# Four Strassen pairs instead of three in the last projection of an encoder trunk, two of each pair's weight sums made by adding DMA transfers

## The chip, the cores and the metric

One core of a Trainium2 chip runs the whole program. The metric is device time in microseconds of one launch, the median of several runs. TensorE (PE) multiplies, VectorE (DVE) and ScalarE (ACT) do the element-wise work, GpSimd (POOL) and SyncE (SP) issue transfers here, and 16 DMA engines carry them out.

## The reference, cut to what matters

Two layers, 256 tokens, model width 2048, all in float32. Each layer projects the normed input into conv, differential-attention and memory-attention heads, and projects the gated head outputs back:

```python
for l in range(DEPTH):                       # DEPTH = 2
    h = rmsnorm(x, norm_g[l])
    proj = h @ w_in[l]
    ...
    y = jnp.concatenate([y_a, y_d, y_m], axis=-1) @ w_out[l]   # (256 x 2048) @ (2048 x 2048)
    x = x + y
```

The last line but one, for l = 1, is where the change works. y has 16 column groups of 128: 0 to 5 from the conv, 6 to 11 from six differential heads, 12 to 15 from four memory heads.

## The kernel before

**Products.** float32 products are made of parts: every weight and every token tile is split into a rounded part (hi, on ScalarE) and a remainder (lo, on VectorE), and a product is three matmuls, hi x hi, hi x lo and lo x hi (lines 301 to 307, 348 to 351). Tokens are the stationary side, in two tiles of 128; 512 weight columns stream. A weight tile of two row blocks by 512 columns (512 KB) is loaded on SP's queue into one of four raw buffers and split into one of four pairs of hi and lo buffers (`load_w`, 286 to 296); it feeds 2 row blocks x 2 token tiles x 3 = 12 matmuls.

**The last projection.** w_out has four column blocks of 512. Blocks 0 and 1 run first over the head groups, with their accumulators left open (1222), and then over the six conv groups (1244 to 1247). Blocks 2 and 3 are done together: `near` accumulates block 2, `far` block 3 (1253, 1291, 1293).

**The Strassen pairs.** For a pair of row blocks k and k+1, two token tiles and the column blocks 2 and 3, the 2 x 2 x 2 product is done with seven products instead of eight (Winograd's form). The four token sums are made ahead by `token_sums` (353 to 366), on VectorE, once the heads that they need are there (`all_sums`, 1203 to 1209). `seven` (368 to 409) loads the two row blocks, each over both column blocks (128 x 1024, 512 KB), on SP; splits B11; makes four weight sums in place on VectorE (line 380, four calls); splits each side; and issues the products. Three go into accumulators that the ordinary tiles share (`near` twice, `far` once), four into accumulators of their own (`x`), which `collect` (1256 to 1280) adds up after the last pair, in steps between later weight tiles. Layer 0 has two pairs; layer 1 has three, ahead of the near block's tiles at positions 2, 6 and 8 of ten remaining row blocks (1249). In layer 1 all weight sums live in the buffers tagged "sh" and "e".

**Order.** Instructions passed to `pin` stay in program order among themselves on their engine; the others are placed by a scheduler at compile time. Each engine then runs its instructions in that fixed order, and so does each queue. `run_side` steps the side tasks once for each weight tile; `later(g, n)` makes a task due n such steps on. `leave(1)` adds column block 1's accumulators to the residual; it is called from inside the first pair (`meanwhile`), and the far accumulators use the same four PSUM buffers in rotation, so they wait for it.

**Buffers that the change takes.** "bgT" holds the conv's gate until the last conv group is multiplied by it (1170); "mqT" and "ga" hold the conv's turned input (1157); "bgx" its source sheet; "mv" the memory values.

Of the kernel before, what the change touches and what calls it, by code (L numbers as in the profile page):

```python
# [10 lines left out]
F32 = mybir.dt.float32  # L11
# [3 lines left out]
ALU = mybir.AluOpType  # L15
# [33 lines left out]
def encoder(ctx: ExitStack, tc: tile.TileContext, x, mem, norm_g, w_in, conv_w, conv_b,  # L49
# [21 lines left out]
    def nm(s):  # L71
        uid[0] += 1
        return f"{s}_{uid[0]}"
# [235 lines left out]
    def block(stat, w, cols, order, steps=1, apart=0, acc=None, more=False, rows=row_tiles, ready=None,  # L309
              opened=None, between={}):  # L310


        opened = opened or (acc is not None,) * NT
        if acc is None:
            acc = accumulators()
        n = len(order)

        def ends(k, t):
            return k == order[0] and not opened[t], k == order[-1] and not more

        late = []
        for c in range(0, n, CK):
            if c in between:
                between[c](acc)
            k0 = order[c]
            parts = ready(c // CK) if ready else load_w(rows(w, k0), cols)
            for j in range(CK):
                k = k0 + j
                settle(stat, k)
                for t in range(NT):  # L330
                    if t > 0 and c >= n - apart:
                        late.append((t, k, *parts[j]))
                    else:
                        products(stat, acc[t], t, k, *parts[j], *ends(k, t))
            run_side(steps)
        whole = late[:-SPLIT] if apart else late
        for t, k, hi, lo in whole:
            products(stat, acc[t], t, k, hi, lo, *ends(k, t))
        if apart:
            near, far = slice(0, NB // 2), slice(NB // 2, NB)  # L340
            for t, k, hi, lo in late[-SPLIT:]:
                products(stat, acc[t][:, near], t, k, hi[:, near], lo[:, near], *ends(k, t))
            acc.append(ps_acc.tile([P, NB // 2], F32, tag="acc", name=nm("rest")))
            for i, (t, k, hi, lo) in enumerate(late[-SPLIT:]):
                products(stat, acc[-1], t, k, hi[:, far], lo[:, far], i == 0, i == SPLIT - 1)
        return acc

    def product(left, acc, right, first, last):

        for i, (a, b) in enumerate(((0, 0), (0, 1), (1, 0))):  # L350
            nc.tensor.matmul(acc, left[a], right[b], start=first and i == 0, stop=last and i == 2)  # L351

    def token_sums(stat, k, home):

        f = tmp.tile([P, 2, SEQ], F32, tag="nat", name=nm("f"), bufs=3)
        pin(nc.vector.tensor_tensor(f, stat[:, 0, k:k + 2, :].bitcast(F32), stat[:, 1, k:k + 2, :].bitcast(F32), ALU.add))
# [3 lines left out]
        pin(nc.vector.tensor_tensor(s[:, 0], a21, a22, ALU.add))  # L360
        pin(nc.vector.tensor_tensor(s[:, 2], a11, a21, ALU.subtract))
        pin(nc.vector.tensor_tensor(s[:, 1], s[:, 0], a11, ALU.subtract))
        pin(nc.vector.tensor_tensor(s[:, 3], a12, s[:, 1], ALU.subtract))
        yield 1
        pin(nc.scalar.copy(home[:, 0], s))
        pin(nc.vector.tensor_tensor(home[:, 1], s, home[:, 0].bitcast(F32), ALU.subtract))

    def seven(stat, k, sums, w, col0, c_near, c_far, x, first, last, homes, meanwhile):


        a, b = (pl.tile([P, 2, NB], F32, tag=tag, name=nm("wide")) for pl, tag in homes)
        for j, raw in enumerate((a, b)):
            pin(nc.sync.dma_start(raw.rearrange("p j c -> p (j c)"), w[(k + j) * P:(k + j + 1) * P, col0:col0 + 2 * NB]))

        def split(src, to=None):
            hi, lo = to or parts_tiles()
            return ((hi, pin(nc.scalar.copy(hi, src))), (lo, pin(nc.vector.tensor_tensor(lo, src, hi.bitcast(F32), ALU.subtract))))  # L377

        def minus(dst, v, u):
            pin(nc.vector.tensor_tensor(dst, v, u, ALU.subtract))  # L380

        def side_of(parts, j):
            return [v[:, j] for v, _ in parts]

        one = keep.tile([P, 2, 1, NB], F32R, tag="mga", name=nm("one"))
        b11 = split(a[:, 0:1], (one[:, 0], one[:, 1]))
        minus(a[:, 0], a[:, 1], a[:, 0])
        minus(a[:, 1], b[:, 1], a[:, 1])
        b2 = split(b)
        minus(b[:, 1], b[:, 1], a[:, 0])  # L390
        minus(b[:, 0], b[:, 0], b[:, 1])
        meanwhile()
        t13 = split(a)
        t42 = split(b)

        def tokens(j, t):
            return [stat[:, part, k + j, t * P:(t + 1) * P] for part in range(2)]

        def summed(i):
            return [sums[:, part, i] for part in range(2)]  # L400

        x1, x5, x6, x7 = x
        product(tokens(0, 0), x1, side_of(b11, 0), first, last)
        product(tokens(1, 0), c_near[0], side_of(b2, 0), False, False)
# [3 lines left out]
        product(tokens(1, 1), c_near[1], side_of(t42, 0), False, False)  # L408
        product(summed(1), x6, side_of(t42, 1), first, last)

    def row_stats(ss, tag):
# [651 lines left out]
    for l in range(DEPTH):  # L1063
# [137 lines left out]
        sums = []  # L1201

        def all_sums(l, yT, sums):
            for n, tag in enumerate(("mkT0", "v") if l + 1 < DEPTH else ("mkT0", "mkT1", "v")):
                while tag == "v" and (l, MH // 2 - 1) not in summed_heads:
                    yield 1
                sums.append(keep.tile([P, 2, 4, P], F32R, tag=tag, name=nm("sums")))
                yield from token_sums(yT, CG + 2 * n, sums[n])
                yield 1
# [29 lines left out]
        def leave(b, acc, keep_order=lambda i: i, n=5):  # L1239
            finish(b, acc, keep_order)  # L1240
            if not final:
                tasks.append(later(x_next(xT, l + 1, b), n))

        for b in range(2):
            block(yT, w_out[l], [(b * NB, NB)], convs, acc=accs[b])
            if b == 0:
                leave(b, accs[b])

        places = (2, 6, 8) if final else (2, 6)
        paired = [CG + 2 * n for n in range(len(places))]  # L1250
        homes = [((tmp, tag),) * 2 for tag in ("sh", "e", "sh")] if final else [((tmp, "sh"),) * 2, ((keep, "bgx"), (keep, "ga"))]
        rest = [k for k in heads + convs if not CG <= k < CG + 2 * len(places)]
        near, far = accumulators(), accumulators()
        x = [pl.tile([P, NB], F32, tag=tag, name=nm("x")) for pl, tag in ((ps_s, "s"), (ps_s, "s"), (ps_t, "t"), (ps_t, "t"))]

        def collect(near):

            def at(t, b):
                return xs[:, t, b * NB:(b + 1) * NB]

            def plus(dst, v, u):
                pin(nc.vector.tensor_tensor(dst, v, u, ALU.add))

            x1, x5, x6, x7 = x
            u, v = (tmp.tile([P, NB], F32, tag="nat", name=nm("u"), bufs=3) for _ in range(2))
            pin(nc.scalar.copy(u, x1))
            plus(at(0, 2), u, at(0, 2))
            plus(u, u, x6)
            plus(v, u, x7)
            yield 1  # L1270
            plus(at(1, 2), v, at(1, 2))
            if not final:
                leave(2, near, n=3)
            plus(u, u, x5)
            plus(at(0, 3), u, at(0, 3))
            yield 1
            plus(v, v, x5)
            plus(at(1, 3), v, at(1, 3))
            if final:
                leave(2, near)  # L1280

        def pair_at(n):
            def run(near):
                seven(yT, paired[n], sums[n], w_out[l], 2 * NB, near, far, x, n == 0, n == len(paired) - 1,
                      homes[n], (lambda: leave(1, accs[1], pin, 4)) if n == 0 else lambda: None)
                if n == len(paired) - 1:
                    tasks.append(later(collect(near), 5))
                run_side(1)
            return run

        block(yT, w_out[l], [(2 * NB, NB)], rest, acc=near, opened=(False, False),
              between={c: pair_at(n) for n, c in enumerate(places)})
        acc = block(yT, w_out[l], [(3 * NB, NB)], rest, apart=4 if final else 0, acc=far, opened=(True, False))
        leave(3, acc)
# [31 lines left out]
```

## Time and profile before

| what | us |
|---|---|
| runs (three): median; lowest to highest | 918.98; 918.62 to 919.94 |
| the profiled execution: whole time | 919.16 |
| the profiled execution: span from first to last instruction | 917.4 |
| TensorE busy in the span | 911.9 |
| VectorE busy | 720.1 |
| ScalarE busy | 515.8 |
| GpSimd busy | 38.3 |

Matmuls overlap one another: each shows about 0.39 us, while a new one starts every 0.23 us, so the pace is read from long unbroken rows and not from single durations. Times in rows of a timeline are microseconds from the start of the span; a row gives start, length, engine, line, operation, output and inputs, shapes, count, and in brackets the idle time before it with what ended it.

### The profile page before, as it was taken

To read this page: it belongs to the slowest core of one execution; us is meant where nothing else is said; L and a number is where in the kernel's file an instruction comes from. 1 tells how busy PE (TensorE), PEld (TensorE's weight loads), DVE (VectorE), ACT (ScalarE), POOL (GpSimd) and SP (SyncE) were. 2 spreads that over 40 slices of the span, in tenths; PEclk is the share of its full clock that TensorE was granted. 3 is DMA by queue.
4 is the path that set the end of the run, shared out by engine and by line. 5 is a ranking of instruction groups with operands and counts; after the bars stand their busy time and mean duration, and the time that the engine had idled before them with its cause. 6 is when DMAs were issued, how large, how long until landed. Compare 5 with 4: busy or idle time off the path is not lost.

```text
span 917.4 us, 12407 instructions
## 1 busy us (share of the span) xinstructions
PE 911.9 (99%) x4161; PEld 757.3 (83%) x4161; DVE 720.1 (78%) x1293; ACT 515.8 (56%) x798; POOL 38.3 (4%) x68
## 2 busy tenths in 40 slices
PE   9999999999999999999999999999999999999998
PEld 6888888888888888888888888888888888888887
DVE  5579978857799697677789857878898787588786
ACT  5667645675555556445556544578555565546352
POOL 2435010000000000000000000000000000000000
PEclk9999999999999999999999999999999999999999
DMA  8899878886679998979777867986889998968842
GB/s 288 289 243 248 287 247 229 244 222 197 188 206 238 247 256 235 263 243 241 264 215 228 275 203 213 268 239 178 236 231 221 266 260 227 268 215 234 275 161 92
DMA packets 244560, 215.15 MB, mean 235 GB/s; under 512 B 131976, under 2 KB 171720, under 8 KB 244496
## 3 DMA queue, kind: packets, MB, share of 16 engines
q1 hardware_dynamic: 239520, 208.71, 79.3%
q0 software_dynamic: 3776, 4.59, 2.1%
q10 hardware_dynamic: 1200, 1.07, 0.3%
q8 instruction: 32, 0.52, 0.2%
q14 instruction: 32, 0.26, 0.1%
HBM read 193.30 MB, written 21.00 MB: 234 GB/s over the span
## 4 chain that ended last, share of the span: by engine, by line
PE 99%; DMA 0%; ACT 0%; SPq 0%; DVE 0%; issue 0%; ACTq 0%
PE acc L305 92%; PE x L351 2%; PE po L519 1%; PE acc L351 1%; PE s L627 1%; PE po L749 1%; PE s L626 1%; PE acc L933 1%; PE pt L763 0%; DMA raw<-in_w_mem_kv_dram 0%; PE s L683 0%; PE s L681 0%; PE s L682 0%; PE rest L305 0%; ACT hi L915 0%; SPq L833 0%
## 5 line engine op out<-in xcount | busy, mean ns | idle before, releaser
L305 PE MATMUL acc<-hi,xT 128*128 128x512 f32 x1792 | 558.4, 390 | 0.0
L294 ACT CAST hi<-raw 128x1024 fp32r<-128x1024 f32 x270 | 283.9, 1053 | 277.3 <-PE acc L305 200.0
L295 DVE TENSOR_TENSOR lo<-raw,hi 128x1024 fp32r<-128x1024 f32 x270 | 329.0, 1222 | 126.7 <-ACT hi L294 124.5
L305 PEld LDWEIGHTS acc<-hi,xT 128*128 128x128 f32 x1792 | 336.3, 188 | 69.0
L305 PE MATMUL acc<-lo,xT 128*128 128x512 f32 x896 | 349.2, 390 | 0.0
L305 PEld LDWEIGHTS acc<-lo,xT 128*128 128x128 f32 x896 | 168.2, 188 | 33.6
L305 PE MATMUL acc<-hi,yT 128*128 128x512 f32 (+1 forms) x432 | 134.1, 388 | 0.0
L305 PEld LDWEIGHTS acc<-hi,yT 128*128 128x128 f32 x432 | 81.0, 188 | 16.7
L305 PE MATMUL acc<-lo,yT 128*128 128x512 f32 x216 | 83.7, 388 | 0.0
L305 PE MATMUL acc<-hi,memT 128*128 128x512 f32 x248 | 78.0, 392 | 0.0
L305 PEld LDWEIGHTS acc<-hi,memT 128*128 128x128 f32 x248 | 46.2, 188 | 9.3
L916 DVE SCALAR_TENSOR_TENSOR lo<-raw,cva,hi 128x1024 fp32r<-128x1024 f32 (+1 forms) x34 | 41.0, 1218 | 15.4 <-ACT hi L915 15.1
L305 PE MATMUL acc<-lo,memT 128*128 128x512 f32 x124 | 48.0, 391 | 0.0
L305 PEld LDWEIGHTS acc<-lo,yT 128*128 128x128 f32 x216 | 40.6, 188 | 8.4
L915 ACT ACTIVATE hi<-raw,cva 128x1024 fp32r<-128x1024 f32 (+1 forms) x34 | 36.5, 1101 | 12.4 <-DMA raw<-in_w_mem_kv_dram 12.2
L305 PEld LDWEIGHTS acc<-lo,memT 128*128 128x128 f32 x124 | 23.3, 188 | 5.5 <-DVE lo L916 0.8
L377 ACT CAST hi<-wide 128x1024 fp32r<-128x1024 f32 x15 | 15.6, 1050 | 16.3 <-DVE wide L380 6.9
L637 ACT ACTIVATE e<-e,mx 128x256 f32<-128x256 f32 x48 | 23.8, 500 | 1.4 <-DVE mx L633 1.3
L780 POOL DMA_DIRECT2D xt<-in_x_dram x32 | 21.5, 678 | 19.7 <-DVE rsy L189 13.6
L377 DVE TENSOR_TENSOR lo<-wide,hi 128x1024 fp32r<-128x1024 f32 x15 | 18.1, 1220 | 3.5 <-ACT hi L377 3.3
L264 ACT ACTIVATE xT<-xf,gx 128x256 fp32r<-128x256 f32 x32 | 14.3, 503 | 5.7 <-DVE xf L786 5.0
L631 DVE SCALAR_TENSOR_TENSOR e<-dist,s 128x512 f32<-128x512 f32 x24 | 15.7, 680 | 2.2 <-PE s L627 1.7
(210 smaller groups left out, 765.8 us busy)
## 6 DMA issues: line engine op xcount, KB each, us to landing
raw<-in_w_in_dram SPq DMA_DIRECT2D x192, 512.0 KB, 4.6
raw<-in_w_out_dram SPq DMA_DIRECT2D x54, 512.0 KB, 4.8
raw<-in_w_in_dram SPq DMA_DIRECT2D x64, 256.0 KB, 4.3
raw<-in_w_mem_kv_dram SPq DMA_DIRECT2D x30, 512.0 KB, 6.4
d<-sh SPq DMA_DIRECT2D x88, 128.0 KB, 4.2
sh<-d SPq DMA_DIRECT2D x72, 128.0 KB, 4.1
wide<-in_w_out_dram SPq DMA_DIRECT2D x10, 512.0 KB, 7.0
xs<-in_x_dram SPq DMA_DIRECT2D x4, 512.0 KB, 6.3
```

The lines of the kernel that those rows point to most:

```text
L264: both = (nc.scalar.activation(hi, src, AF.Copy, scale=gain), nc.vector.scalar_tensor_tensor(lo, src, gain, hi.bitcast(F32), ALU.mult, ALU ...
L294: nc.scalar.copy(hi, raw)
L295: nc.vector.tensor_tensor(lo_, raw, hi.bitcast(F32), ALU.subtract)
L305: i = nc.tensor.matmul(acc, left, right, start=start, stop=stop)
L351: nc.tensor.matmul(acc, left[a], right[b], start=first and i == 0, stop=last and i == 2)
L377: return ((hi, pin(nc.scalar.copy(hi, src))), (lo, pin(nc.vector.tensor_tensor(lo, src, hi.bitcast(F32), ALU.subtract))))
L519: nc.tensor.matmul(po[:, t, :], eT[:, i, t, k, :], v[:, k, h * P:(h + 1) * P], start=k == 0, stop=k == NT - 1)
L631: nc.vector.scalar_tensor_tensor(e[:, c], dist, -slopes[h], s[c], ALU.mult, ALU.add)
L637: nc.scalar.activation(e[:, c, i], e[:, c, i], AF.Exp, bias=mx[:, c, i:i + 1], accum_out=sm[:, c, i:i + 1])
L780: tc.keep_in_program_order(nc.gpsimd.dma_start(st[:, n], src[n * B:(n + 1) * B].rearrange("p (b r) -> b p r", b=NA)))
L915: both = (nc.scalar.activation(hi[:, j], raw[:, j], AF.Copy, scale=g), nc.vector.scalar_tensor_tensor(lo[:, j], raw[:, j], g, hi[:, j].bit ...
L916: nc.vector.scalar_tensor_tensor(lo[:, j], raw[:, j], g, hi[:, j].bitcast(F32), ALU.mult, ALU.subtract))
```

## The change

- **Signs.** In both layers the token sums and the weight sums change sign, so that all four weight sums are additions: B11 + B12, B12 + B22, B22 + (B11 + B12), B21 + (B22 + B11 + B12). `collect` subtracts where it added.
- **Adding transfers, layer 1 only.** A new function `load_pair` loads a pair. In layer 1 it also copies B11 to a place of its own on SP's queue, and GpSimd issues a transfer of B12 and B22 that adds them to the loaded B11 and B12. `seven` then makes only two sums there.
- **A fourth pair, layer 1 only**: row blocks 12 and 13, the first two memory heads, whose token sums go to "mv". The pairs stand at positions 0, 2, 4 and 6 of eight remaining row blocks.
- **Earlier loads, layer 1 only.** The first pair's loads stand ahead of column block 1's conv tiles; each pair loads the next one's. The buffers are "sh", "e", "bgx" and "ga", and "sh" again; the copies of B11 go to "bgT" and "mqT".
- **Order inside the first pair.** It opens the near accumulators, and `leave(1)` comes after the splits of the sums instead of ahead of them. `collect` is due three steps after the last pair, not five.

```diff
 def token_sums(stat, k, home):
...
-        pin(nc.vector.tensor_tensor(s[:, 0], a21, a22, ALU.add))
+        pin(nc.vector.tensor_tensor(s[:, 0], a21, a22, ALU.subtract))
...
-        pin(nc.vector.tensor_tensor(s[:, 3], a12, s[:, 1], ALU.subtract))
+        pin(nc.vector.tensor_tensor(s[:, 3], a12, s[:, 1], ALU.add))
...
-    def seven(stat, k, sums, w, col0, c_near, c_far, x, first, last, homes, meanwhile):
-        a, b = (pl.tile([P, 2, NB], F32, tag=tag, name=nm("wide")) for pl, tag in homes)
+    def load_pair(k, w, col0, homes):
+
+        a, b = (h[:, 0:2] for h in homes[:2])
         for j, raw in enumerate((a, b)):
             pin(nc.sync.dma_start(raw.rearrange("p j c -> p (j c)"), w[(k + j) * P:(k + j + 1) * P, col0:col0 + 2 * NB]))
+        if len(homes) > 2:
+            pin(nc.sync.dma_start(homes[2][:, 0], w[k * P:(k + 1) * P, col0:col0 + NB]))
+            pin(nc.gpsimd.dma_start(a, w[k * P:(k + 2) * P, col0 + NB:col0 + 2 * NB].rearrange("(j p) c -> p j c", p=P),
+                                    accum_op=ALU.add))
+
+    def seven(stat, k, sums, c_near, c_far, x, first, last, opens, homes, meanwhile):
...
-        b11 = split(a[:, 0:1], (one[:, 0], one[:, 1]))
-        minus(a[:, 0], a[:, 1], a[:, 0])
-        minus(a[:, 1], b[:, 1], a[:, 1])
+        b11 = split(homes[2] if len(homes) > 2 else a[:, 0:1], (one[:, 0], one[:, 1]))
+        if len(homes) == 2:
+            plus(a[:, 0], a[:, 0], a[:, 1])
+            plus(a[:, 1], a[:, 1], b[:, 1])
         b2 = split(b)
-        minus(b[:, 1], b[:, 1], a[:, 0])
-        minus(b[:, 0], b[:, 0], b[:, 1])
-        meanwhile()
+        plus(b[:, 1], b[:, 1], a[:, 0])
+        plus(b[:, 0], b[:, 0], b[:, 1])
+        if not opens:
+            meanwhile()
         t13 = split(a)
         t42 = split(b)
+        if opens:
+            meanwhile()
...
-            for n, tag in enumerate(("mkT0", "v") if l + 1 < DEPTH else ("mkT0", "mkT1", "v")):
-                while tag == "v" and (l, MH // 2 - 1) not in summed_heads:
+            for n, tag in enumerate(("mkT0", "v") if l + 1 < DEPTH else ("mkT0", "mkT1", "v", "mv")):
+                while tag in ("v", "mv") and (l, MH // 2 - 1) not in summed_heads:
...
+        places = (0, 2, 4, 6) if final else (2, 6)
+        paired = [CG + 2 * n for n in range(len(places))]
+        rest = [k for k in heads + convs if not CG <= k < CG + 2 * len(places)]
+        copies = []
+
+        def homes(n):
+            def home(pl, tag, j=2):
+                return pl.tile([P, j, NB], F32, tag=tag, name=nm("wide"))
+
+            ab = (home(keep, "bgx", 3), home(keep, "ga", 3)) if n == len(paired) - (2 if final else 1) else \
+                [home(tmp, "e" if final and n == 1 else "sh") for _ in range(2)]
+            if not final:
+                return ab
+            if n == 0:
+                copies.extend((home(keep, "bgT", 3), home(keep, "mqT")))
+            return *ab, copies[n // 3][:, n % 3:n % 3 + 1]
+
+        loaded = []
+
+        def load_next():
+            if len(loaded) < len(paired):
+                loaded.append(homes(len(loaded)))
+                load_pair(paired[len(loaded) - 1], w_out[l], 2 * NB, loaded[-1])
+
         for b in range(2):
+            if final and b:
+                load_next()
             block(yT, w_out[l], [(b * NB, NB)], convs, acc=accs[b])
...
-        places = (2, 6, 8) if final else (2, 6)
-        paired = [CG + 2 * n for n in range(len(places))]
-        homes = [((tmp, tag),) * 2 for tag in ("sh", "e", "sh")] if final else [((tmp, "sh"),) * 2, ((keep, "bgx"), (keep, "ga"))]
-        rest = [k for k in heads + convs if not CG <= k < CG + 2 * len(places)]
...
-            plus(u, u, x5)
+            minus(u, x5, u)
...
-            plus(v, v, x5)
+            minus(v, x5, v)
...
         def pair_at(n):
             def run(near):
-                seven(yT, paired[n], sums[n], w_out[l], 2 * NB, near, far, x, n == 0, n == len(paired) - 1,
-                      homes[n], (lambda: leave(1, accs[1], pin, 4)) if n == 0 else lambda: None)
+                load_next()
+                seven(yT, paired[n], sums[n], near, far, x, n == 0, n == len(paired) - 1,
+                      places[n] == 0, loaded[n], (lambda: leave(1, accs[1], pin, 4)) if n == 0 else lambda: None)
                 if n == len(paired) - 1:
-                    tasks.append(later(collect(near), 5))
+                    tasks.append(later(collect(near), 3 if final else 5))
...
-        block(yT, w_out[l], [(2 * NB, NB)], rest, acc=near, opened=(False, False),
+        block(yT, w_out[l], [(2 * NB, NB)], rest, acc=near, opened=(places[0] == 0,) * NT,
               between={c: pair_at(n) for n, c in enumerate(places)})
```

More of the change, by code (lines that the diff above doesn't have):

```diff
@@ L366, in token_sums @@
         pin(nc.vector.tensor_tensor(home[:, 1], s, home[:, 0].bitcast(F32), ALU.subtract))
-    def seven(stat, k, sums, w, col0, c_near, c_far, x, first, last, homes, meanwhile):
-        a, b = (pl.tile([P, 2, NB], F32, tag=tag, name=nm("wide")) for pl, tag in homes)
+    def load_pair(k, w, col0, homes):
+        a, b = (h[:, 0:2] for h in homes[:2])
         for j, raw in enumerate((a, b)):
             pin(nc.sync.dma_start(raw.rearrange("p j c -> p (j c)"), w[(k + j) * P:(k + j + 1) * P, col0:col0 + 2 * NB]))
+        if len(homes) > 2:
[3 more added lines that the diff above has]
+    def seven(stat, k, sums, c_near, c_far, x, first, last, opens, homes, meanwhile):
+        a, b = (h[:, 0:2] for h in homes[:2])
         def split(src, to=None):
@@ L377, in split, with plus @@
             return ((hi, pin(nc.scalar.copy(hi, src))), (lo, pin(nc.vector.tensor_tensor(lo, src, hi.bitcast(F32), ALU.subtract))))
-        def minus(dst, v, u):
-            pin(nc.vector.tensor_tensor(dst, v, u, ALU.subtract))
+        def plus(dst, v, u):
+            pin(nc.vector.tensor_tensor(dst, v, u, ALU.add))
         def side_of(parts, j):
@@ L403, in seven @@
         product(tokens(0, 0), x1, side_of(b11, 0), first, last)
-        product(tokens(1, 0), c_near[0], side_of(b2, 0), False, False)
+        product(tokens(1, 0), c_near[0], side_of(b2, 0), opens, False)
         product(summed(3), c_far[0], side_of(b2, 1), first, False)
@@ L407, in seven @@
         product(summed(2), x7, side_of(t13, 1), first, last)
-        product(tokens(1, 1), c_near[1], side_of(t42, 0), False, False)
+        product(tokens(1, 1), c_near[1], side_of(t42, 0), opens, False)
         product(summed(1), x6, side_of(t42, 1), first, last)
@@ L1262, in plus, with minus @@
                 pin(nc.vector.tensor_tensor(dst, v, u, ALU.add))
+            def minus(dst, v, u):
+                pin(nc.vector.tensor_tensor(dst, v, u, ALU.subtract))
             x1, x5, x6, x7 = x
```

## Prediction

> **What bounds the kernel now.** I read the page's busy shares and its chain of waits first, then the windows of the end of layer 1, which is where the change works.
>
> ```profile
> span 917.4 us, 12407 instructions
> ...
> PE 911.9 (99%) x4161; PEld 757.3 (83%) x4161; DVE 720.1 (78%) x1293; ACT 515.8 (56%) x798; POOL 38.3 (4%) x68
> ...
> PE 99%; DMA 0%; ACT 0%; SPq 0%; DVE 0%; issue 0%; ACTq 0%
> ```
>
> TensorE is busy for 911.9 of 917.4 us, and the chain that ended last is TensorE for 99%. Only 5.5 us of the span lie outside it. An average can hide a stage, so here is the stage (columns: window, length, then busy time and count for PE, PEld, DVE, ACT, POOL, then granted clock, DMA share, GB/s):
>
> ```profile
> 860.00:870.00 10.00, 10.00 (x46) 8.29 (x45) 8.28 (x12) 3.69 (x4) 0.00 (x0) 1.00 1.00 316
> 870.00:880.00 10.00, 10.00 (x45) 8.24 (x45) 7.73 (x12) 5.59 (x6) 0.00 (x0) 1.00 0.77 259
> 880.00:890.00 10.00, 10.00 (x46) 8.26 (x45) 9.44 (x12) 4.73 (x5) 0.00 (x0) 1.00 0.39 139
> 890.00:900.00 10.00, 10.00 (x46) 8.17 (x45) 9.59 (x10) 6.70 (x7) 0.00 (x0) 1.00 0.32 98
> 910.00:918.00 8.00, 3.81 (x26) 3.33 (x24) 1.94 (x5) 0.00 (x0) 0.00 (x0) 0.96 0.20 66
> ```
>
> Through the three pairs (874 to 897 us) TensorE has no gap. VectorE stands at 9.4 and 9.6 of 10: near the limit, but not over it. So there is no stall that the change could remove; its gain is the matmuls that it drops, and its risk is a stall that it creates.
>
> **Part 1: the fourth pair, matmuls.** The pace comes from one unbroken run of the chain, the pairs' count from the window of the pairs' line, the end from the chain's last pieces.
>
> ```profile
> 806.71 68.04 PE acc L305 x300
> 874.75 0.69 PE x L351 x3
> 912.73 1.09 PE rest L305 x9
> 864.00:912.00 48.00, 15.91 (x63) 11.83 (x63) 1.00 0.49 157
> ```
>
> 68.04 / 300 = 0.2268 us for a 512-column matmul. A pair has seven products of three matmuls, 21 (63 for three pairs). The same two row blocks in the ordinary way cost 2 row blocks x 2 token tiles x 2 column blocks x 3 = 24. So the fourth pair removes 3 matmuls: 3 x 0.2268 = **-0.68 us**. Nothing hides this: the chain is TensorE to the end.
>
> **Part 2: VectorE and ScalarE in the pairs.**
>
> ```profile
> L377 ACT CAST hi<-wide x9: 1044/1052/1057, 866.7 to 892.6; 128x1024 fp32r<-128x1024 f32 x9
> L377 DVE TENSOR_TENSOR lo<-wide,hi x9: 1217/1218/1226, 868.2 to 893.7; 128x1024 fp32r<-128x1024 f32 x9
> L380 DVE TENSOR_TENSOR wide<-wide x6: 691/692/693, 866.9 to 891.8; 128x512 f32<-128x512 f32 x6
> L377 ACT CAST one<-wide x3: 612/620/621, 864.9 to 886.5; 128x512 fp32r<-128x512 f32 x3
> DMA to landing us min/median/max: 4.5/6.2/8.7
> ```
>
> ```profile
> 871.39 1.44 DVE L1230 TENSOR_TENSOR xs<-acc,xs 128x256 f32<-128x256 f32 x4 [0.53 <-PE acc L305]
> 879.14 0.69 DVE L377 TENSOR_TENSOR one<-wide,one 128x512 fp32r<-128x512 f32 x1
> 883.79 2.50 DVE L377 TENSOR_TENSOR lo<-wide,hi 128x1024 fp32r<-128x1024 f32 x2
> ```
>
> The second pair's VectorE work runs from 879.14 to 883.79 + 2.50 = 886.29, 7.15 us. Two of its four sums leave: 7.15 - 2 x 0.69 = 5.77. With the weight tile that follows each pair (1.22, a split of the same size) a period is 6.99 us of VectorE, 0.62 + 4 x 1.05 = 4.8 of ScalarE, and 33 matmuls x 0.2268 = 7.48 of TensorE. Before, the same period was 7.15 + 1.22 = 8.37 on VectorE and lived on a lead from the single tiles between; now four pairs follow at every second row block, and VectorE still gains 0.5 us in each. I cost it at nothing: TensorE covers it.
>
> The first pair moves to the head of its block. TensorE then ends the second column block's accumulation at T0 = 874.59 - 12 x 0.2268 = 871.87 (row below; twelve matmuls stood between) and after six of the pair's matmuls, at T0 + 1.36, wants the accumulator that L1230 has to empty. Those four additions take 1.44 us; the two for the first tile can start when its matmuls end, 0.68 before T0, so 0.72 us of work has 2.0 us of room. They now stand behind the pair's last splits on VectorE instead of ahead of them; the four buffers of split weights let these run before T0. Queued behind the additions is the next tile's split, 1.22 us, which TensorE wants 21 matmuls (4.8 us) after T0. Bounds: 0 to 1.44 us, if that cover is gone; I take 0, by the 0.53 us that VectorE itself waited at this place.
>
> The fourth token sum adds six VectorE instructions and a ScalarE copy, like the third's:
>
> ```profile
> 817.36 0.69 DVE L356 TENSOR_TENSOR f<-yT 128x512 f32<-128x512 f32 x1
> 819.94 0.28 DVE L360 TENSOR_TENSOR sums<-f 128x128 f32<-128x128 f32 x1
> 822.66 0.68 DVE L366 TENSOR_TENSOR sums<-sums,sums 128x512 fp32r<-128x512 f32 x1
> 824.24 1.23 DVE L295 TENSOR_TENSOR lo<-raw,hi 128x1024 fp32r<-128x1024 f32 x1 [0.89 <-ACT hi L294]
> 826.96 1.23 DVE L295 TENSOR_TENSOR lo<-raw,hi 128x1024 fp32r<-128x1024 f32 x1 [1.50 <-ACT hi L294]
> ```
>
> 0.69 + 4 x 0.28 + 0.68 = 2.5 us of VectorE. Before the splits right behind it VectorE stood idle for 0.89 and 1.50 us, and it was ahead of TensorE, which has no gap there. Nothing, or 2.5 if no lead were there. The signs turned over cost nothing in either layer: addition and subtraction are one instruction here.
>
> **Part 3: the loads.** Per pair of layer 1 there are now the two wide loads, one copy of 256 KB on SP, and one adding transfer of 512 KB issued by POOL, which waits for the first wide load; POOL has no other work here (0.00 in every window above).
>
> ```profile
> 838.67 17.07 SPq L291 DMA_DIRECT2D raw<-in_w_out_dram  x8
> 855.79 0.94 SPq L373 DMA_DIRECT2D wide<-in_w_out_dram  x2
> 850.85 0.42 DVE L1170 TENSOR_TENSOR z<-z,bgT 128x256 f32<-128x256 f32 x1
> 874.59 0.86 PE L351 MATMUL x<-one,yT 128*128 128x512 f32 x3
> ```
>
> ```profile
> DMA packets 244560, 215.15 MB, mean 235 GB/s; under 512 B 131976, under 2 KB 171720, under 8 KB 244496
> ...
> q1 hardware_dynamic: 239520, 208.71, 79.3%
> q0 software_dynamic: 3776, 4.59, 2.1%
> ...
> raw<-in_w_out_dram SPq DMA_DIRECT2D x54, 512.0 KB, 4.8
> ...
> sh<-kd POOLq DMA_DIRECT2D x2, 512.0 KB, 6.1
> ```
>
> SP issues a weight tile every 2.4 us, well ahead of use: the eighth of that run, at about 855.4 and just ahead of the first pair's loads at 855.79, is the tile that TensorE begins at T0. The first pair's loads now stand four tiles earlier, at about 846 to 848. The copy goes into the tile bgT, which VectorE reads until 851.27; if SP stands there, the next raw tile leaves 3.1 us late (851.3 against 848.2), lands 4.8 later at 856.1, is split by 858.6, and TensorE wants it at T0 - 36 x 0.2268 = 863.7. Hidden by 5 us.
>
> No row here has an adding transfer. Its nearest is POOL's plain 512 KB, 6.1 us (lower bound: it can't be below the plain wide load's 4.5); as it also reads what it adds to, I take twice, **12.2 us**, and as upper bound four times, 24.4. Deadlines, with the slowest wide landing of 8.7 and 2.5 us for split and remainder (1.05 + 1.22 and two handovers), the first summed weights being needed nine matmuls, 2.04 us, into a pair: first pair 871.87 + 2.04 - 2.5 - (848 + 8.7) = 14.7 us for the transfer; second, loaded by 855.4: 14.8; third, loaded behind it, more. The fourth can't be loaded until the first pair's buffers are read, about T0: 871.87 + 3 x 7.48 + 2.04 - 2.5 - (871.87 + 8.7) = **13.3 us**, the tightest. 12.2 fits by 1.1: nothing.
>
> The Trainium skill, "Collectives: The Full Stack", section "The bandwidth ceiling: the fold count and why AG ≠ RS ≠ AR", says that an adding DMA runs at half the rate of a copy because it reads two sources, not because adding costs time. By it the transfer is twice a plain one and the sum stays -0.68; no trace here shows it. The Trainium skill, "DMA: Bandwidth & Descriptors", section "Anatomy of one DMA — SWDGE (gpsimd) path", gives 2.0 us plus bytes at 436 GB/s; for 1 MB of reads that is an estimate of 4.4 us, and the same sum; no run shown so far has such a transfer.
>
> Bytes: from 846 to the last near tile's split (871.87 + 22.4 = 894.3) go seven raw tiles (3.7 MB) and four pairs at 1.05 + 0.26 + 0.52 MB (7.3 MB), 11.0 MB in 48.3 us, 228 GB/s; 271 with the adding counted twice. The window from 860 shows 316. It fits.
>
> **The sum.** -0.68 and nothing else. The end stays as it is: the collecting steps come at the first, second and third tile of the far block instead of the third to fifth, and TensorE still has its last matmuls after them.
>
> ```profile
> 913.84 0.42 DVE L1232 TENSOR_TENSOR xs<-rest,xs 128x256 f32<-128x256 f32 x1 [0.32 <-PE rest L305]
> ```
>
> From this addition to the span's end go 917.4 - 913.84 = 3.6 us, untouched. The profiled execution took 919.16 (1.76 outside its span): 919.16 - 0.68 = 918.48. It lies 0.18 above the median of the runs, 918.98, so the median forecast is **918.3**.
>
> **The rivals.**
>
> *The adding transfer is late* (slower). Place: the fourth pair, whose ScalarE split of summed weights waits for POOL's transfer; in order behind it stand the other splits of that pair and of the next tile, so TensorE runs dry. It decides from 13.3 us on; slower by 0.2% needs 13.3 + 0.68 + 1.84 = 15.8. At three times the plain 6.1, 18.3 us, it is 5.0 late at that pair: 923.3. At 24.4, 11.1: 929.4, the earlier pairs' lateness being contained in it only in part. For it: the operation is not in the trace, and small-packet q0 traffic takes 2.1% of the engines for 4.59 MB against 79.3% for 208.71, 1.2 times as long per byte. Against: the slack of 13 to 15 us. Chance 0.13.
>
> *The burst of loads starves the raw tiles* (slower). All of the first three pairs' 5.5 MB is asked for between 846 and 858, with four raw tiles among it. At the 316 GB/s of the 860 window, adding counted twice, the 5.5 + 1.6 + 2.1 MB take 29 us, to 875; the second near tile, asked for at 858 behind them, has its split buffer from T0 + 7.48 = 879.4 on. At the whole span's mean of 235 GB/s it would be 39 us, to 885, 5.6 late: 923.9. Chance 0.07.
>
> *A small new wait eats the gain*: the additions at the head (up to 1.44) or the sums (part of 2.5), net 0 to +1.8, so 918.98 to 920.8. For it: VectorE near full. Chance 0.07.
>
> *More than the matmuls is saved*: the relief on VectorE or the earlier collecting shortens the end. It would have to find 1.2 us in the 3.6 us tail or the 1.9 us at the start, which hang on the last matmuls and the first load. Below 917.1. Chance 0.05.
>
> **How the numbers follow.** The forecast has the remaining 0.68, own range 917.6 to 919.2. A measurement of this kernel tells 0.2% (1.84 us) from no change; the gain is 0.07%, so faster is 0.05, within is 0.68 + 0.07 = 0.75, slower 0.13 + 0.07 = 0.20. The range reaches from 917.3 to 922.0, leaving out the late transfer's upper part and most of the last case.
>
> **What would show it.** In the changed profile: 3 matmuls fewer, 84 on the products' line in layer 1; no TensorE gap from 860 to 900; POOL's four transfers landing in 6 to 13 us; no subtraction of weights on VectorE in layer 1 beyond two a pair; the last matmul near 913.1. Wrong if ScalarE's splits of summed weights stand behind a POOL transfer and TensorE behind them, if raw tiles land later than 10 us, or if an idle TensorE appears at the head of the third column block.

## The result, and the profile after

Slower: 930.02 us (929.06 to 930.94, four runs) against 918.8 (918.28 to 919.94, four runs), a ratio of 1.012 with a 95% interval of 1.0103 to 1.0138. The profiled execution of the changed kernel has a span of 926.9 us. Its page, the busy shares and the chain of waits by engine:

```profile
PE 915.3 (99%) x4158; PEld 759.3 (82%) x4158; DVE 721.2 (78%) x1297; ACT 517.0 (56%) x801; POOL 43.1 (5%) x72
...
PE 97%; DMA 2%; ACT 0%; DVE 0%; issue 0%; ACTq 0%
```

The three matmuls are gone (4158 for 4161), yet DMA has 2% of the chain, where it had 0%. Two windows of the end of layer 1 (columns as before) say where; in the others TensorE is busy throughout:

```profile
870.00:880.00 10.00, 3.94 (x12) 2.13 (x10) 2.39 (x3) 1.96 (x3) 3.70 (x3) 0.80 0.80 194
880.00:890.00 10.00, 9.30 (x29) 7.46 (x30) 9.85 (x14) 6.14 (x7) 1.18 (x1) 0.69 1.02 268
```

TensorE is busy for 3.94 us of the first ten, and the granted clock (the third number from the end of a row) falls to 0.80 and 0.69. TensorE's timeline there, which is the first pair:

```profile
871.00 0.39 PE L305 MATMUL acc<-hi,yT 128*128 128x512 f32 x1
875.25 0.50 PE L351 MATMUL x<-one,yT 128*128 128x512 f32 x1 [3.86 <-ACT one L385]
875.97 1.20 PE L351 MATMUL x<-one,yT 128*128 128x512 f32 x2 [0.23 <-DVE one L385]
...
880.70 1.22 PE L351 MATMUL x<-hi,sums 128*128 128x512 f32 x2 [2.68 <-ACT hi L385]
...
885.57 0.63 PE L305 MATMUL acc<-hi,yT 128*128 128x512 f32 x1
885.99 0.53 PE L351 MATMUL x<-lo,sums 128*128 128x512 f32 x1
886.36 0.39 PE L351 MATMUL x<-hi,sums 128*128 128x512 f32 x1
```

TensorE waits for ScalarE's splits, of B11 (`one`) and of the first summed weights (`hi`). From the start at 871.00 to the one at 886.36 there are 19 steps, which at 0.2268 us would take 4.31; they took 15.36, so 11.05 us are lost. Up to the first matmul of the summed weights (880.70) six steps take 9.70 us in place of 1.36: 8.34 lost, of which 3.86 + 0.23 + 2.68 = 6.77 are idle time. From there thirteen steps take 5.66 us in place of 2.95: 2.71 lost to matmuls that start 0.42 to 0.43 us apart (885.57 to 885.99) in place of 0.23. With the 0.68 that the dropped matmuls give back, 10.4 in all. The chain's pieces confirm it: from the first to the last row below TensorE took 116.44 us, before 912.73 - 806.71 = 106.02, 10.42 more.

```profile
806.07 49.01 PE acc L305 x216
...
857.49 9.51 DMA raw<-in_w_out_dram
867.01 6.34 DMA wide<-in_w_out_dram
873.39 6.07 DMA wide<-in_w_out_dram
...
922.51 1.09 PE rest L305 x9
```

So the chain goes through the first pair's wide loads and the adding transfer that POOL issued at 873.39. It adds into the first of the two loads, issued at 865.67, which by the trace's records landed at 872.66 (the chain names the second, by its time). These loads are late. SP's timeline, with VectorE's row of the additions of column block 0:

```profile
852.42 0.93 SPq L372 DMA_DIRECT2D wide<-in_w_out_dram  x2
...
855.14 0.98 SPq L372 DMA_DIRECT2D wide<-in_w_out_dram  x2
...
863.36 1.19 SPq L1247 DMA_DIRECT2D out_dram<-xs  x2
865.67 1.68 SPq L372 DMA_DIRECT2D wide<-in_w_out_dram  x2
868.50 0.33 SPq L374 DMA_DIRECT2D wide<-in_w_out_dram  x1
```

```profile
862.77 1.41 DVE L1242 TENSOR_TENSOR xs<-acc,xs 128x256 f32<-128x256 f32 x4
```

The loads at 852.42 and 855.14 are the second and third pairs'. The first pair's leave at 865.67, behind two stores of column block 0 (L1247), and these wait for the additions of 862.77. All these loads are pinned, and the later pairs' overtook the first pair's, so a pin does not keep pinned instructions in order among themselves, other than said under Order.

The stores are not the whole delay. SP had issued both by 864.55 (863.36 + 1.19); the two loads and the copy then leave at 865.67, 867.01 and 868.50, each within 0.02 us of the landing of an earlier transfer that reports on the same semaphore in the trace's records (the third pair's copy, then the weight tiles issued at 857.49 and 860.21). This is the chain's step from `raw` to `wide`. It makes the first load 1.1 us later.

POOL, which issues in order with the first pair's transfer at the head, issues three in a row from 873.39; the second pair's leaves 15 us after its wide loads had landed (874.15 against 859.05, by the trace's records). ScalarE's split of B11 waits for the copy of 868.50:

```profile
874.58 0.62 ACT L385 CAST one<-wide 128x512 fp32r<-128x512 f32 x1 [12.98 <-DMA wide<-in_w_out_dram]
```

**Theory (order):** a pinned instruction stays behind whatever was traced just ahead of it on its engine, pinned or not. The last on SP before `load_next()` are the stores of `leave(0)`, so the first pair's loads come after column block 0 has ended. The later pairs' loads were traced behind a weight tile, and leave right behind one. **Rival (adding):** the adding transfers take too long, or fill the DMA engines, wherever the loads stand. A third part, the **clock**, follows from either: the gaps lower it, and that costs by itself.

### The profile page after: what moved, and what is told of

It is laid out like the page before. It is cut to its first block, busy times and chain, and to the rows that moved or that the text cites. A ratio compares the mean times of both kernels' runs of the same rounds, so it can differ in the third digit from the quotient of the medians.

```text
span 926.9 us, 12427 instructions
## 1 busy us (share of the span) xinstructions
PE 915.3 (99%) x4158; PEld 759.3 (82%) x4158; DVE 721.2 (78%) x1297; ACT 517.0 (56%) x801; POOL 43.1 (5%) x72
## 3 DMA queue, kind: packets, MB, share of 16 engines
q1 hardware_dynamic: 239840, 209.76, 78.8%
## 4 chain that ended last, share of the span: by engine, by line
PE 97%; DMA 2%; ACT 0%; DVE 0%; issue 0%; ACTq 0%
PE acc L305 88%; PE x L351 2%; PE acc L351 1%; DMA wide<-in_w_out_dram 1%; PE po L531 1%; DMA raw<-in_w_out_dram 1%; PE s L639 1%; PE po L761 1%; PE s L638 1%; PE acc L945 0%; PE pt L775 0%; PE s L695 0%; PE s L693 0%; PE s L694 0%; PE warm L128 0%; DVE lo L295 0%
## 5 line engine op out<-in xcount | busy, mean ns | idle before, releaser
L305 PE MATMUL acc<-hi,yT 128*128 128x512 f32 (+1 forms) x416 | 129.8, 388 | 0.0
L305 PEld LDWEIGHTS acc<-hi,yT 128*128 128x128 f32 x416 | 78.2, 188 | 16.1
L305 PE MATMUL acc<-lo,yT 128*128 128x512 f32 x208 | 80.6, 388 | 0.0
L375 POOL DMA_DIRECT2D wide<-in_w_out_dram x4 | 4.9, 1589 | 758.7 <-DMA wide<-in_w_out_dram 758.7
L385 ACT CAST hi<-wide 128x1024 fp32r<-128x1024 f32 x18 | 18.8, 1049 | 14.4 <-DVE wide L388 8.0
L385 DVE TENSOR_TENSOR lo<-wide,hi 128x1024 fp32r<-128x1024 f32 x18 | 21.9, 1222 | 2.6 <-ACT hi L385 2.3
```

The source lines that it names most:

```text
L305: i = nc.tensor.matmul(acc, left, right, start=start, stop=stop)
```

## The experiments

### Where the first pair's loads stand

**e1_loads_before_stores** calls `load_next()` ahead of the stores:

```diff
         for b in range(2):
-            if final and b:
-                load_next()
             block(yT, w_out[l], [(b * NB, NB)], convs, acc=accs[b])
             if b == 0:
+                if final:
+                    load_next()
                 leave(b, accs[b])
```

> Theory (order): the first pair's loads are late because they are kept in program order behind whatever SP was given before them, and that is the two stores of column block 0, which wait for VectorE's additions. Here they are traced ahead of those additions, behind the last conv tile. It expects the first wide load issued at about 846 to 848 us instead of 865.67, POOL's first adding transfer before 860 instead of at 873.39, no gap of TensorE and a granted clock of 1.00 through the pairs, and 918.3 us (917.8 to 919.0). Rival (adding transfer): POOL's transfers themselves are late; POOL still starts late or lands after 871, and the time stays above 922. Rival (density): four pairs at every second tile are too much for VectorE; TensorE still waits for splits, 920 or more.

Measured: 922.6 us (five runs; before 918.76), ratio 1.0041, 1.0028 to 1.0053. 7.4 us came back, but the time is 3.6 us above the order theory's 917.8 to 919.0 and above 922, as the adding rival had it. SP's first row of the pair and POOL's first transfer stand where the forecast had them:

```profile
845.21 0.94 SPq L372 DMA_DIRECT2D wide<-in_w_out_dram  x2
```

```profile
851.93 1.25 POOL L375 DMA_DIRECT2D wide<-in_w_out_dram  x1 [725.80 <-DMA wide<-in_w_out_dram]
```

**e2_stores_on_act** leaves the trace order and takes the stores off SP:

```diff
-                        eng = nc.scalar if lo else nc.sync
+                        eng = nc.scalar if lo or b == 0 else nc.sync
```

> The loads stay where the changed kernel has them; only column block 0's two stores on SP go to ScalarE's queue, so that the last thing on SP ahead of the loads is a weight tile. Order: as good as moving the loads, 918.3 us (917.6 to 919.2), first wide load before 850. Adding transfer or density: no difference from the changed kernel, about 930.

Measured: 923.36 us in a single run, again above the forecast; the first wide loads leave at 845.22. Two edits that share nothing but that no store stands ahead of these loads on SP's queue move them by 20 us and give back some 7 us each.

**e3_no_adding** keeps the change's order and makes all four sums on VectorE; there are no copies and no adding transfers:

```diff
-            if not final:
-                return ab
-            if n == 0:
-                copies.extend((home(keep, "bgT", 3), home(keep, "mqT")))
-            return *ab, copies[n // 3][:, n % 3:n % 3 + 1]
+            return ab
```

> The changed kernel with the four sums of layer 1 on VectorE: no copies of B11, no adding transfers; the order of the loads is unchanged. Order: the first pair's loads still leave at about 865.7 and land at about 872 to 873, TensorE stands for 2 to 5 us ahead of the first pair and runs some matmuls at the lower clock, 922 to 927 us. Adding transfer: with none there is nothing late, 918.3 to 920.

Measured: 927.26 us (four runs), 1.009, 1.0076 to 1.0103, 0.3 us above the order theory's 922 to 927. Without any adding transfer 8.5 of the 11 us stay, and the wait is the same one:

```profile
PE x L351 <- ACT one L385: 2.3, 1, 2.3
```

**e4_no_adding_early** is e3 with e1's order.

> Four pairs, all sums on VectorE, the first loads traced ahead of column block 0's additions. It prices what the adding transfers are for. Order: no late load; VectorE needs 8.37 us a period against TensorE's 7.48, 0.9 too much in each of three periods, with some 2 us of lead, so 918.3 to 920. Density: 920 to 923, with TensorE waiting for splits in the third and fourth pair.

Measured: 918.48 us (eleven runs; before 918.76), 0.9995, 0.9986 to 1.0005. So the order alone, without adding transfers, is worth 927.26 - 918.48 = 8.8 us, and in the early order the adding with its copies of B11 (e1 against e4) costs 4.1: the order theory holds for the larger part, but the adding has a part of its own.

### The 4 us that e1 keeps

In e1 the first pair runs without a gap; the second has two, 1.39 and 1.24 us. Counted from start to start the loss is larger: from the chain's start of the block to its last matmuls e1 takes 916.25 - 806.90 = 109.35 us, against 105.40 in f1 below. The chain of waits of e1 goes through these pieces:

```profile
806.90 43.57 PE acc L305 x192
...
864.42 15.02 DMA raw<-in_w_out_dram
...
879.51 2.53 DMA out_dram<-xs
...
916.25 1.09 PE rest L305 x9
```

and ScalarE's and VectorE's timelines there are

```profile
879.51 0.82 ACTq L1247 DMA_DIRECT2D out_dram<-xs  x2
880.45 0.62 ACT L385 CAST one<-wide 128x512 fp32r<-128x512 f32 x1 [7.09 <-DMA out_dram<-xs]
```

```profile
873.44 1.41 DVE L1242 TENSOR_TENSOR xs<-acc,xs 128x256 f32<-128x256 f32 x4
```

The two stores of column block 1 on ScalarE's queue had their data at 874.85 (873.44 + 1.41), but were issued only at 879.51, 0.08 us after a weight tile, issued at 864.42, had landed. Nothing joins the two but the semaphore on which both report that they have landed: in the trace's records it is the same one, ScalarE's wait for it ends 0.03 us after the tile's landing, and the same pair of instructions shares one again in e2, f2 and f1. Behind the stores, in order on ScalarE, waits the second pair's split of B11, whose copy had landed at 864.98. The weight tile itself took 15 us because the DMA engines were full, as the windows of e1 show (the DMA share is the last number but one):

```profile
850.00:860.00 10.00, 10.00 (x46) 8.29 (x45) 5.31 (x8) 4.52 (x5) 1.25 (x1) 1.00 0.97 301
860.00:870.00 10.00, 10.00 (x45) 8.27 (x45) 6.68 (x10) 2.62 (x3) 2.39 (x2) 1.00 1.05 373
870.00:880.00 10.00, 9.73 (x43) 7.70 (x41) 4.82 (x7) 3.05 (x3) 0.00 (x0) 1.00 1.08 318
```

Three runs take this apart; all start from e1. **f1_stores_off_act** moves the stores, and leaves the backlog:

```diff
-                        eng = nc.scalar if lo else nc.sync
+                        eng = nc.scalar if lo and b != 1 else nc.sync
```

> With the loads early (the first experiment) 3.8 us over the kernel before remain. In its trace ScalarE stands 7.09 us ahead of the second pair's split of B11, whose copy had landed 15 us earlier; the instruction in front of it in ScalarE's queue is a store of column block 1, which waits for the completion semaphore that it shares with a weight tile issued at 864.42 and landed at 879.43. Here these two stores go to SP's queue instead. Theory (shared semaphore in front of the splits): TensorE's gaps of 1.4 and 1.2 us go, 918.3 us (917.8 to 919.2). Rival (data late): the second pair's adding transfer and the DMA engines' backlog are what it waits for; no difference from 922.6, or another wait at the same place, above 921.

Measured: 918.19 us (eleven runs; before 918.95 of 21), 0.9993, 0.9984 to 1.0001. The windows of f1, its split of B11 on ScalarE, and its wide loads' landing times:

```profile
870.00:880.00 10.00, 10.00 (x46) 8.21 (x45) 8.30 (x12) 5.61 (x7) 0.00 (x0) 1.00 1.08 323
880.00:890.00 10.00, 10.00 (x46) 8.21 (x45) 9.82 (x11) 7.64 (x9) 1.18 (x1) 1.00 0.89 249
```

```profile
873.40 0.62 ACT L385 CAST one<-wide 128x512 fp32r<-128x512 f32 x1
```

```profile
DMA to landing us min/median/max: 3.9/9.9/15.6
```

The engines are as full and the longest landing is 15.6 us, but the split comes at 873.40 instead of 880.45, and TensorE has no gap. The store itself is as late as before: SP issues it at 879.70, again 0.06 us after the landing of the tile that shares its semaphore. Only what was queued behind the store has changed.

**f2_loads_spread** means to thin the backlog: each further pair's loads are traced one weight tile later.

```diff
+        def next_pair():
+            load_next()
+            return
+            yield
...
-                load_next()
+                if not final:
+                    load_next()
...
+                if final:
+                    tasks.append(later(next_pair(), 1))
```

> With the loads early, each further pair's loads are traced one weight tile later, so that two pairs are not asked for at once. The stores stay on ScalarE. Backlog theory: the longest landing falls from 15.0 to under 11 us, the store then finds its semaphore free, 918.3 to 919.5 us. If the backlog comes from the bytes themselves (adding transfers at twice a copy's cost), landings stay at 13 us or more and the time at 921 to 923.

Measured: 922.37 us (five runs), 1.0035, 1.0022 to 1.0049, a miss: a tile is only 12 x 0.2268 = 2.7 us, the longest landing of a weight tile is still 15.0, and the wait is the same. ScalarE's row of the split in f2 names the weight tile itself:

```profile
881.33 0.62 ACT L385 CAST one<-wide 128x512 fp32r<-128x512 f32 x1 [7.80 <-DMA raw<-in_w_out_dram]
```

**f3_copies_no_adding** is e1 with the copies of B11, and the sums on VectorE:

```diff
-            pin(nc.gpsimd.dma_start(a, w[k * P:(k + 2) * P, col0 + NB:col0 + 2 * NB].rearrange("(j p) c -> p j c", p=P),
-                                    accum_op=ALU.add))
...
-        if len(homes) == 2:
+        if True:
```

> With the loads early and the copies of B11 kept, but the sums on VectorE again: no adding transfer. It tells the copies' traffic from the adding transfers'. Adding transfers make the backlog: longest landing at most 11 us, no gap of TensorE beyond 0.5 us, 918.3 to 919.5. Copies make it: 920.5 to 922.5.

Measured: 918.53 us (ten runs), 0.9993, 0.9984 to 1.0002. Wide loads land within 10.4 us and weight tiles within 10.1, the stores of column block 1 are issued on ScalarE at 872.06 and 872.49, and TensorE has no gap in the pairs. So it is the adding transfers' own traffic, not the copies, that makes the backlog; the backlog costs only through the store. And the two additions that they take off VectorE in each pair are worth nothing: f3, e4 and f1 can't be told apart.

### The clock

**g1_clock_kept** is the changed kernel with matmuls of zeros into x1 in the first gap, whose result the product that follows overwrites:

```diff
         x1, x5, x6, x7 = x
+        if opens:
+            for _ in range(20):
+                pin(nc.tensor.matmul(x1, zeros[:, 0:P], zeros, start=True, stop=True))
```

> The changed kernel with 20 matmuls of zeros on TensorE just ahead of the first pair (4.5 us at 0.227), into the accumulator that the pair's first product opens anew. They fill the 3.86 us that it stands for the copy of B11 and change nothing of the loads. Of the 10.2 us that the changed kernel loses from the head of its third column block on, I put 6.8 to standing and 4.2 to the first pair's 21 matmuls at 0.427 instead of 0.227 us. Theory (the clock falls because TensorE stood): the granted clock stays at 1.00 in 870 to 890 unless the second gap of 2.7 us alone lowers it, and the time is about 926.4 us (925.5 to 927.5). Rival (all of it is late data, the slow matmuls only wait for their operands): no change or a little longer, 930 to 931.

Measured: 929.89 us (four runs; before 918.99), 1.0118, 1.0101 to 1.0135, a miss. TensorE's timeline of g1:

```profile
871.95 4.49 PE L417 MATMUL x<-zeros 128*128 128x512 bf16 x20
876.56 0.49 PE L351 MATMUL x<-one,yT 128*128 128x512 f32 x1
...
882.00 1.22 PE L351 MATMUL x<-hi,sums 128*128 128x512 f32 x2 [3.53 <-ACT hi L385]
...
887.26 0.39 PE L351 MATMUL x<-lo,sums 128*128 128x512 f32 x1
```

The second gap, 3.53 us here, lowers the clock without the first: the twelve steps from 882.00 to 887.26 take 5.26 us, not 2.72. The run does show what the clock cost behind the first gap: nothing. From the first matmul of B11 to the first of the summed weights go 882.00 - 876.56 = 5.44 us here, with fast matmuls and the longer gap, and 880.70 - 875.25 = 5.45 in the changed kernel, with slow ones and 2.68. Both wait for the adding transfer, which the slow matmuls do not delay. What the clock costs behind the second gap this run leaves open.

**g3_clock_kept_twice** fills the second as well:

```diff
+        if opens:
+            left, right = summed(3), side_of(b2, 1)
+            nc.tensor.matmul(c_far[0], left[0], right[0], start=first, stop=False)
+            for _ in range(15):
+                pin(nc.tensor.matmul(x5, zeros[:, 0:P], zeros, start=True, stop=True))
...
```

> The changed kernel with the 20 matmuls of zeros ahead of the first pair, and 15 more (3.4 us by the 4.49 us that the 20 took) in the second gap, ahead of the first product of x5; nothing else differs. In the trace of the kernel with the first 20 alone TensorE stood 3.53 us in the second gap and eleven matmuls after it started 0.427 us apart, not 0.227. Clock theory (a gap of about 3 us is enough by itself, and the slow matmuls are on the path): all matmuls of the first pair 0.227 us apart, granted clock 1.00 in 880 to 890, and 11 x 0.2 = 2.2 us less than with the first 20 alone: 927.3 to 927.9. Rival (the pair waits for its sums in any case, so the slow matmuls fill time that would be waited): 929.5 to 930.2, with new idle time on TensorE between the products of the first pair.

Measured: 927.46 us (five runs; before 919.49), 1.0085, 1.0071 to 1.0099, which doesn't overlap g1's interval. Its window and timeline:

```profile
880.00:890.00 10.00, 9.67 (x42) 7.04 (x40) 9.84 (x14) 6.04 (x7) 1.08 (x1) 1.00 1.03 245
```

```profile
877.25 3.41 PE L424 MATMUL x<-zeros 128*128 128x512 bf16 x15
```

The gaps are filled with zeros, the clock stays at 1.00, and the medians differ by 2.4 us. The same twelve steps, 880.77 to 883.72 here, take 2.95 us instead of g1's 5.26, which is 2.3 less. In the two profiled executions the summed weights also come 1.0 us earlier (880.77 - 806.59 from the block's start, against 882.00 - 806.79), which is not the clock's doing; how much of that is in the medians stays open. The clock after the second gap is a cost of its own, near the 2.71 of the account above.

**g2_late_stores_off_act** is f1's edit of the stores on the change's own late order.

> The changed kernel's late loads, with column block 1's stores on SP's queue as in the experiment that gave 918.19. It asks whether that edit helps without the early loads. Order theory: what the first pair waits for is its own loads, 865.67 to 874.55, and POOL's transfer; the store is not in front of them, so 929 to 931. If the store on ScalarE's queue were the whole cause: 918 to 920.

Measured: 928.71 us (four runs), 1.0103, 1.0088 to 1.0118, not to be told from the change. Where the first pair is late, ScalarE's stores aren't what it waits for; f1 needs both edits.

## Why the prediction was wrong

**The failed step is in Part 3: "The first pair's loads now stand four tiles earlier, at about 846 to 848".** That is where the call stands in the code. The chip issued them at 865.67, behind the stores of column block 0, of which the prediction says nothing. With e1's order they leave at 845.21. The first pair's deadline, 14.7 us for the adding transfer, was reckoned from 848; the arithmetic behind it was sound, its starting point was 18 us off, and no slack was left. The prediction followed the added wait (for bgT, "Hidden by 5 us") and not what else stood on SP ahead of the moved loads.

**Not priced at all: the clock.** Of the 11.05 us lost, 8.34 are the wait for the summed weights; behind it matmuls ran at half their rate, which cost 2.71 by the trace; g3, with the clock kept, gets 2.3 of it back. The step missing is the clock in the price of a stall.

**Nor the wait for a semaphore.** Part 3 lets a transfer leave when its queue reaches it. In the trace it also waits for the last transfer that used its semaphore: 1.1 us for the first pair's load in the change, and 7.09 us of ScalarE in e1, where f1 is 4.4 us faster.

**Part 1 held.** f1 has the whole change in the order that was forecast, with two stores on another queue, and its chain reads

```profile
806.04 65.32 PE acc L305 x288
...
911.44 1.09 PE rest L305 x9
```

911.44 - 806.04 = 105.40 us against 106.02 before: -0.62, for a forecast of -0.68. Its 918.19 us is near the forecast's 918.3, but the gain is too small for the intervals: those of f1, f3 and e4 all include 1.

**Part 2 held.** In f1 VectorE stands at 8.30 and 9.82 of 10 from 870 to 890 and TensorE has no gap; even with all four sums on it (e4: 9.70 and 9.81 in the same windows) there is none. The head of the block, the token sums and the order of the additions cost nothing, as reckoned.

**The adding transfer's duration held, inside its bounds.** Issue to landing, KB each and median us, plain wide loads and adding transfers of the changed kernel:

```profile
wide<-in_w_out_dram SPq DMA_DIRECT2D x12, 512.0 KB, 6.4
...
wide<-in_w_out_dram POOLq DMA_DIRECT2D x4, 512.0 KB, 7.6
```

In f1 they are 7.7 and 9.9, the longest adding transfer 11.6. 12.2 had been taken, with 13.3 as the tightest deadline. The rival that the adding transfer is late at the fourth pair fell: it was late at the first, for its start and not its length. That this rival's time at 24.4 us, 929.4, lies near the measured 930.02 is chance.

**"It fits", of the bytes, was half right.** In the forecast's order the engines are full from 850 to 880 and tiles land after 15 us, nearer to the rival of the burst (9.2 MB to 875 at 316 GB/s) than to the sum. That rival looked for the price in TensorE waiting for raw tiles. TensorE did not wait for one; the price came through a store that shared a late tile's semaphore, a wait of 7.09 us on ScalarE, and it showed in e1, e2 and f2. In the change the first pair's loads come later, and ScalarE's splits wait for those.

## What to carry to other kernels

When a transfer is moved in the code, read what stands ahead of it on its queue at the new place, above all stores that wait for results, and take its issue time from there; a pin keeps it behind them. Look also for an earlier transfer that uses the same completion semaphore: here each such transfer had to land first. A transfer issued on an engine that also computes can hold that engine's work for something unrelated, so keep stores off it while the DMA engines are full. And price a TensorE stall of two microseconds or more with a clock that may fall behind it.

## What had not been expected of the hardware

**A window of the clock need not be idle as a whole for the clock to fall.** In the trace's records the granted clock changes only on a grid of 3.41 us and goes down to 0.50 (in the changed kernel from 876.03 to 886.27, three windows). After 2.28 us of idle time (e3) and 2.02 (e2) matmuls started 0.43 us apart; after 2.13 (f2) they did not. TensorE's row after the gap and two windows of that grid (columns as before), of e2 and then of f2:

```profile
881.76 0.49 PE L351 MATMUL x<-one,yT 128*128 128x512 f32 x1 [2.02 <-ACT one L385]
...
879.54:882.95 3.41, 1.16 (x4) 0.60 (x4) 0.95 (x2) 1.86 (x3) 1.12 (x1) 1.00 1.02 385
882.95:886.37 3.42, 3.42 (x10) 2.36 (x8) 3.35 (x4) 1.55 (x2) 0.06 (x1) 0.50 1.05 285
```

```profile
882.00 0.50 PE L351 MATMUL x<-one,yT 128*128 128x512 f32 x1 [2.13 <-ACT one L385]
...
877.70:881.11 3.41, 2.18 (x10) 1.48 (x8) 0.00 (x0) 0.00 (x0) 0.00 (x0) 1.00 0.99 334
881.11:884.53 3.42, 2.30 (x8) 1.39 (x9) 2.26 (x3) 2.52 (x3) 1.18 (x1) 1.00 0.92 290
```

e2's gap lies in one window, in which TensorE was busy for 1.16 us, and the next window runs at 0.50. f2's gap is cut by the edge of a window, TensorE was busy for 2.18 and 2.30 us in the two, and the clock stays at 1.00. In the other traces with gaps the same holds: 1.27 us busy or less (g1 1.27, e3 0.92, the changed kernel 0.56) brought the clock down, 2.17 or more (e1) did not. Where between 1.27 and 2.17 the limit lies isn't shown.

The Trainium skill, "TensorE: Matmul & The Clock Gate", section "What's actually happening", gives a half-rate state after at least one idle window of about 3.4 us, with windows that run free of the kernel. The half rate (0.43 us for 512 columns), the window's length and its running free agree; a window did not have to be wholly idle, as 2.02 us of e2's were enough, so there the runs decide.

**An adding transfer holds the DMA engines about twice as long as a plain one of the same packets.** The queue rows of the changed kernel:

```profile
q1 hardware_dynamic: 239840, 209.76, 78.8%
q0 software_dynamic: 4864, 6.69, 3.4%
```

Queue q0 had 4.59 MB and 2.1% before. The 2.10 MB added take 0.034 x 926.9 - 0.021 x 917.4 = 12.2 us of all 16 engines, 5.8 us per MB; q1's take 730 / 209.76 = 3.5, which is 1.7 times less. But q1's mean holds packets of all sizes, those of 128 bytes at 7.2 us per MB. In the trace's packet records from 850 to 900 us a packet of 2048 bytes takes 194 ns when it adds and 96 ns when it is copied on q1, 2.0 times as long (in f1 179 and 96, 1.9 times). The queue alone does not do it: q0's plain packets of 4096 bytes took 3.2 us per MB from 100 to 800 us, as q1's of 2048. So the measured ratio agrees with the half rate that the prediction cited from "Collectives: The Full Stack" of the Trainium skill, where it stands for the adding step of a collective; the reason given there is not shown by these runs. POOL is busy for 1.59 us with each issue (1.2 in f1, where they don't follow one another).
